# Twenty-four modulation products moved into the last attention pair, the mask made later, W_out staged under z's weights

## The chip, the core and the metric

The kernel runs on one core of a Trainium2 chip. The core has a matrix engine (TensorE, PE in the profile, with its weight loads as PEld), a vector engine (VectorE, DVE), a scalar engine (ScalarE, ACT), a general engine (GpSimd, POOL) and an engine that here only issues transfers (SyncE, SP). They share SBUF, the on-chip memory of 128 partitions; PE writes its results to a second memory, PSUM. Each engine takes its instructions in one fixed order and waits on semaphores where it needs another engine's result.

The metric is the time of one execution on the device, in microseconds. All arithmetic is in 32-bit floating point; a 32-bit matrix product is made here from three products of rounded parts (high times high, high times low, low times high).

## The reference

One layer of a hybrid encoder: 1024 tokens of width 1024. The parts that this case touches:

```python
mod = (c_act @ w_ada[l] + b_ada[l])[:, None, :]
sh_m, sc_m, g_m, sh_f, sc_f, g_f = jnp.split(mod, 6, axis=-1)      # six vectors of 1024
h = rmsnorm(x, norm_mix_w[l]) * (1 + sc_m) + sh_m
z, xbc, dt_raw, q, k, v = jnp.split(h @ w_in[l], IN_SPLITS, axis=-1)
y_ssd = ssd_mixer(z, xbc, dt_raw, ...)       # causal conv of width 4 and silu on xbc, scan in chunks, gate by silu(z), norm
y_att = chunk_attention(q, k, v, rel_bias[l])  # 8 heads of 64: own chunk of 64 tokens and the 8 before it
x = x + g_m * (jnp.concatenate([y_ssd, y_att], axis=-1) @ w_out[l])
h = rmsnorm(x, norm_ffn_w[l]) * (1 + sc_f) + sh_f
x = x + g_f * conv_ffn(h, w_up[l], ffn_conv_w[l], w_down[l])
...
return rmsnorm(x, final_norm_w)
```

The modulation `mod` is a product of a vector with a 1024 x 6144 matrix. The kernel makes it on VectorE, 128 columns at a time: 48 products in all, eight for each of the six vectors.

## The kernel before

The work runs in stages, and the code is written in that order, but the order on each engine is made by a scheduler: it lets work of a later stage slip in wherever buffers allow it by its own estimate of times. What the profile shows is that order.

1. The first 60 us load `x`, make the products for `SC_M` and `SH_M` and normalise. `hth` and `htl` are the rounded high part of h and the rest.
2. Attention runs over four pairs of heads. `qkp` is a pool of 12 tiles of 4 KB a partition; each pair takes six (`q`, `kh`, `kl` for two heads), so pairs 2 and 3 reuse those of 0 and 1. Inside a pair the loop over `u` takes two blocks of 128 queries at a time. `attn_scores` multiplies q with k into an `s` tile (there are two of these), adds the bias and finds the row's extreme on VectorE (L319), exponentiates on ScalarE (L322), takes the reciprocal of the row sum on VectorE (L324) and scales by it on GpSimd (L325). `attn_pv` transposes the result on PE, splits it into `pt` high and low (ScalarE and VectorE, L65 and L66) and multiplies with v; L367 and L368 add the halves up into `ya`.
3. The conv stage. `conv_silu` makes one of eight column tiles of `xbc`: `wu_pair` loads 512 KB of weights into one half of `raws` and splits them (ScalarE `wh`, GpSimd `wl`), `gemm_ft` does 48 products of 512 columns into an `s` tile, and VectorE runs three shifted multiply-adds from it (L415) and two halves of silu (L421). After each of the eight, three modulation products follow by `mods`: `mod_col` loads 512 KB of `w_ada` into one of three `mt` tiles, and VectorE multiplies with the row `rowa` and sums (L114). `tc.issue_after` keeps a product behind the conv's last VectorE instruction. They make `G_M`, `SC_F` and `SH_F`. The last four conv tiles are transposed into `xs` (L488).
4. The z stage: `wz_weights` loads and splits z's weights in two halves of four tiles, and `z_tile` makes 16 tiles of z. Eight more products by `mod_col` (`G_F`) stand ahead of it. Once `rowb` (the gate of the mixer, as a row in every partition) is made, `wout_weights` loads each of eight W_out tiles into `raws`, multiplies it by the gate (the fold, L511; `FOLD` says whether on GpSimd, 0, or VectorE, 1) and splits it into `wh`/`wl` or `woh`/`wol`.
5. The scan over eight chunks (`ssd_chunk`) together with the output product (`wout_tile`), then the feed-forward part from about 600 us to the end.

SP's transfers stand in one queue in program order; one that waits for a buffer holds up all behind it.

Of the kernel before, what the change touches and what calls it, by code (L numbers as in the profile page):

```python
# [10 lines left out]
F32 = mybir.dt.float32  # L11
# [15 lines left out]
PB = (2, 2, 1, 3)  # L27
FOLD = (0, 1, 0, 1)
PRST = 4
MTB = 3  # L30
GP, GPL = {0: (0,1), 2: (2,)}, ()
# [14 lines left out]
def tile_block(ctx: ExitStack, tc: tile.TileContext, x, crep, pk, w_ada, w_first, w_ft, w_z,  # L46
# [250 lines left out]
    def attn_scores(p, i, bt):  # L297
# [12 lines left out]
        for h in range(2):  # L310
            pt_ = p_tile()
            nm, rs = stat(), stat()
            if len(parts) == 1:
                src, bsl, dst = st[h][:, 0:n], bt[h][:, off:off + n], pt_[:, 0:n]
            else:
                src = st[h].rearrange("p (a b) -> p a b", a=2)[:, :, 0:320]
                bsl = bt[h].rearrange("p (a b) -> p a b", a=2)
                dst = pt_.rearrange("p (a b) -> p a b", a=2)
            V.tensor_tensor_reduce(out=dst, in0=src, in1=bsl, scale=-1.0, scalar=3e38,  # L319
                                   op0=ALU.add, op1=ALU.min, accum_out=nm)  # L320
            pv_ = pt_[:, 0:n]
            A.activation(pv_, pv_, AF.Exp, scale=-1.0, bias=nm, accum_out=rs)  # L322
            rr = stat()
            V.reciprocal(rr, rs)  # L324
            G.tensor_scalar(pv_, pv_, rr, None, op0=ALU.mult)  # L325
            res.append(pt_)
        return res

    def attn_pv(p, u, h, p0, p1):
# [12 lines left out]
        while done < nb:  # L342
# [16 lines left out]
            for bi, ((j, c0, n), o) in enumerate(bank):  # L359
# [10 lines left out]
                        tl.rearrange("p (a b) -> p a b", a=2), ALU.add)  # L370

    def attention(p, extra=()):
        extra = dict(extra)
# [7 lines left out]
        for u in range(4):  # L381
            pa = attn_scores(p, 2 * u, bt)
            pb = attn_scores(p, 2 * u + 1, bt)
            for fn in extra.get(u, ()):
                fn()
            for h in range(2):
                attn_pv(p, u, h, pa[h], pb[h])
# [20 lines left out]
    def conv_silu(ft, dst, th2):  # L408
        wh, wl = wu_pair(w_ft[ft], A, G)
        ps = s_tile()  # L410
# [15 lines left out]
    for p in (1, 2):  # L426
        attention(p, {u: [part(p + 1, w) for w in ws] for u, ws in GP.items()})
        for w in GPL:
            gemm_part(p + 1, w)
    attention(3)  # L430
    es_at.close()

# [24 lines left out]
    tle, ones = tle1[:, 0, :], tle1[:, 1, :]  # L457
    sgtr = bcp.tile([P, P], F32R, name="sgtr")
    sgt_ = th512()[:, 0:P]
    G.memset(ones, 1.0)  # L460
# [5 lines left out]
    sgt = f32(sgtr)  # L466
    na = bcp.tile([P, 16], F32, name="na")[:, 0:8]
    es_t = ExitStack()
    es_m = ExitStack()
    mtp = es_m.enter_context(tc.tile_pool(name="mtp", bufs=1, side="right", reuse_waits="tile"))  # L470

    def mt_tile():
        return mtp.tile([P, D], F32, tag="mt", bufs=MTB, name="mt")

    def mods(kt, at):
        for m in (G_M, SC_F, SH_F):
            mod_col(m + kt, mt_tile(), at)

    for g in range(2):
        mods(2 * g, conv_silu(4 + g, bt_[g], th512))  # L480
        mods(2 * g + 1, conv_silu(6 + g, ct_[g], th512))
    for ft in range(4):
        xt = bcp.tile([P, S], F32, tag="rm", bufs=2, name="xst")
        mods(4 + ft, conv_silu(ft, xt, th512))
        for hh in range(2):
            tps = tp_tile()
            for j in range(4):
# [3 lines left out]
                         tps.rearrange("p (a b) -> p a b", a=4), AF.Copy)  # L491
    mod_scale(affn, SC_F, NFFN, 0, KT)
    mod_shift(bffn, SH_F, 0, KT)
    wop_ = []
    halves = [slice(0, 512), slice(512, 1024)]
    order = [4, 5, 6, 7, 0, 1, 2, 3]

    def wout_weights(dh, js):
        ws = []
        for j in js:  # L500
# [14 lines left out]
        return ws  # L515

    es_m.close()

# [772 lines left out]
```

## Time and profile before

| | us |
|---|---|
| median of three runs (lowest, highest) | 1277.99 (1275.63, 1278.07) |
| the profiled execution | 1276.49 |
| its span, first to last instruction | 1274.8 |
| PE busy, share of the span | 1187.0, 93% |
| DVE busy | 960.0, 75% |
| ACT busy | 560.8, 44% |
| POOL busy | 199.0, 16% |
| mean granted PE clock | 0.975 |

The change touches the stretch from about 240 to 480 us: the last attention pair is in it from 244, the conv stage's products start at 274, z's at 395, the scan at 454. An engine that is mostly busy over the whole span can still stand idle in one stage, so the prediction reads this stretch in pieces. In the views of time the columns of each engine are its busy time in the piece and, in brackets, the number of instructions; "PEclk" is the granted clock of PE as a share of full speed.

### The profile page before, as it was taken

To read this page: it belongs to the slowest core of one execution; us is meant where nothing else is said; L and a number is where in the kernel's file an instruction comes from. 1 tells how busy PE (TensorE), PEld (TensorE's weight loads), DVE (VectorE), ACT (ScalarE), POOL (GpSimd) and SP (SyncE) were. 2 spreads that over 40 slices of the span, in tenths; PEclk is the share of its full clock that TensorE was granted. 3 is DMA by queue.
4 is the path that set the end of the run, shared out by engine and by line. 5 is a ranking of instruction groups with operands and counts; after the bars stand their busy time and mean duration, and the time that the engine had idled before them with its cause. 6 is when DMAs were issued, how large, how long until landed. Compare 5 with 4: busy or idle time off the path is not lost.

```text
span 1274.8 us, 15617 instructions
## 1 busy us (share of the span) xinstructions
PE 1187.0 (93%) x5786; PEld 992.2 (78%) x5786; DVE 960.0 (75%) x1448; ACT 560.8 (44%) x917; POOL 199.0 (16%) x178
## 2 busy tenths in 40 slices
PE   5898999999796979999889999999999999999995
PEld 3786888878686968888668888888888888888884
DVE  7927455554887786764989988888988879856976
ACT  4527455653322453423734445344445344433443
POOL 1305463661210242220000000000000000000002
PEclk9999999899897989999989999999999999999998
DMA  9702121100556222112113222333222195834433
GB/s 334 261 19 78 41 71 38 57 1 34 201 195 215 100 83 67 55 54 91 67 67 123 107 78 89 103 121 124 100 95 87 75 329 200 304 109 148 151 131 132
DMA packets 57835, 150.86 MB, mean 118 GB/s; under 512 B 5792, under 2 KB 5920, under 8 KB 56352
## 3 DMA queue, kind: packets, MB, share of 16 engines
q1 hardware_dynamic: 50704, 125.49, 29.2%
q10 hardware_dynamic: 7056, 24.38, 4.8%
q8 instruction: 45, 0.74, 0.2%
q14 instruction: 30, 0.25, 0.1%
HBM read 116.56 MB, written 29.10 MB: 114 GB/s over the span
## 4 chain that ended last, share of the span: by engine, by line
PE 79%; DVE 11%; ACT 4%; DMA 3%; issue 2%; POOL 1%; SPq 0%; DVEq 0%; POOLq 0%; ACTq 0%
PE dn L57 5%; PE dn L56 5%; PE dn L58 5%; PE uY L56 5%; PE uY L58 5%; PE uY L57 5%; PE uZ L56 3%; PE uZ L58 3%; PE uZ L57 3%; PE uX L56 3%; PE uX L57 3%; PE uX L58 3%; PE acc L56 3%; PE acc L57 3%; PE acc L58 3%; PE s L56 2%
## 5 line engine op out<-in xcount | busy, mean ns | idle before, releaser
L762 POOL TENSOR_TENSOR st<-st,mhalf 128x1 f32<-128x1 f32 x16 | 12.4, 777 | 681.6 <-DVE st L761 681.6
L56 PE MATMUL dn<-w 128*128 128x512 f32 x308 | 111.9, 389 | 0.0
L57 PE MATMUL dn<-w 128*128 128x512 f32 x308 | 111.9, 389 | 0.0
L58 PE MATMUL dn<-w 128*128 128x512 f32 x308 | 103.3, 389 | 0.0
L325 POOL TENSOR_SCALAR p<-p,st 128x640 f32<-128x640 f32 (+4 forms) x64 | 94.1, 1486 | 30.1 <-DVE st L324 26.3
L65 ACT ACTIVATE w<-ya 128x1024 fp32r<-128x1024 f32 (+1 forms) x44 | 41.8, 950 | 100.6 <-PE uY L58 93.2
L56 PEld LDWEIGHTS dn<-w 128*128 128x128 f32 x308 | 57.8, 188 | 12.1
L57 PEld LDWEIGHTS dn<-w 128*128 128x128 f32 x308 | 57.8, 188 | 12.1
L58 PEld LDWEIGHTS dn<-w 128*128 128x128 f32 x308 | 57.8, 188 | 11.9
L66 DVE TENSOR_TENSOR pt<-tp,pt 128x512 fp32r<-128x512 f32 (+2 forms) x72 | 41.9, 596 | 28.9 <-ACT pt L65 21.8
L65 ACT ACTIVATE w<-xs 128x1024 fp32r<-128x1024 f32 (+1 forms) x44 | 41.8, 951 | 41.1 <-PE uY L58 31.6
L319 DVE CUSTOM_DVE_ANT_0 p<-s,bias 128x640 f32<-128x640 f32 (+4 forms) x64 | 40.6, 651 | 24.7 <-PE tp L351 8.7
L56 PE MATMUL s<-hth,wh 128*128 128x512 f32 x128 | 51.3, 401 | 7.8 <-DVE ct L415 7.5
L65 ACT ACTIVATE pt<-tp 128x512 fp32r<-128x512 f32 (+2 forms) x72 | 36.4, 523 | 39.2 <-PE tp L351 19.8
L58 PE MATMUL s<-hth,wl 128*128 128x512 f32 x128 | 51.5, 402 | 0.0
L904 DVE SCALAR_TENSOR_TENSOR a<-cv,pkt,a 128x1023 f32<-128x1023 f32 (+1 forms) x40 | 51.1, 1276 | 0.1
L57 PE MATMUL s<-htl,wh 128*128 128x512 f32 x128 | 51.0, 399 | 0.0
L66 DVE TENSOR_TENSOR w<-ya,w 128x1024 fp32r<-128x1024 f32 (+1 forms) x44 | 47.7, 1084 | 4.4 <-ACT w L65 4.4
L322 ACT ACTIVATE p<-p,st 128x640 f32<-128x640 f32 (+4 forms) x64 | 44.1, 690 | 13.1 <-DVE st L319 12.9
L66 POOL TENSOR_TENSOR wl<-raws,wh 128x1024 fp32r<-128x1024 f32 x14 | 34.9, 2496 | 95.6 <-ACT wh L65 93.2
L904 DVE SCALAR_TENSOR_TENSOR a<-cg,pkt,a 128x1023 f32<-128x1023 f32 (+1 forms) x40 | 49.5, 1276 | 0.0
L66 DVE TENSOR_TENSOR w<-xs,w 128x1024 fp32r<-128x1024 f32 (+1 forms) x44 | 47.6, 1082 | 0.3 <-ACT w L65 0.3
(407 smaller groups left out, 3613.5 us busy)
## 6 DMA issues: line engine op xcount, KB each, us to landing
mt<-in_w_ada_dram SPq DMA_DIRECT2D x32, 512.0 KB, 4.5
gz<-a ACTq DMA_DIRECT2D x10, 1024.0 KB, 5.3
adat<-in_w_ada_dram SPq DMA_DIRECT2D x16, 512.0 KB, 5.8
ya<-in_w_up_dram SPq DMA_DIRECT2D x10, 768.0 KB, 4.0
xs<-in_w_up_dram SPq DMA_DIRECT2D x10, 768.0 KB, 4.0
raws<-in_w_ft_dram SPq DMA_DIRECT2D x14, 512.0 KB, 3.5
gy<-a ACTq DMA_DIRECT2D x10, 512.0 KB, 2.6
qk<-in_x_dram SPq DMA_DIRECT2D x8, 512.0 KB, 6.8
```

The lines of the kernel that those rows point to most:

```text
L56: T.matmul(ps, lh, rh, start=start, stop=False, skip_group_check=more)
L57: T.matmul(ps, lh, rl, start=False, stop=False, skip_group_check=more)
L58: T.matmul(ps, ll, rh, start=False, stop=stop, skip_group_check=more)
L65: i = A.activation(hi, src, AF.Copy) if ehi is A else ehi.tensor_copy(hi, src)
L66: return i, elo.tensor_tensor(lo, src, f32(hi), ALU.subtract)
L319: V.tensor_tensor_reduce(out=dst, in0=src, in1=bsl, scale=-1.0, scalar=3e38, op0=ALU.add, op1=ALU.min, accum_out=nm)
L322: A.activation(pv_, pv_, AF.Exp, scale=-1.0, bias=nm, accum_out=rs)
L325: G.tensor_scalar(pv_, pv_, rr, None, op0=ALU.mult)
L762: G.tensor_tensor(r, ms, mhalf[:, 0:1], ALU.pow)
L904: V.scalar_tensor_tensor(a[:, j:S], c[:, 0:S - j], w[2 - j], a[:, j:S], op0=ALU.mult, op1=ALU.add)
```

## The change

- The 24 products of `G_M`, `SC_F` and `SH_F` leave the conv stage. They are done inside `attention(3)`: after the scores of `u` = 1 four, of `u` = 2 four, of `u` = 3 sixteen (`MODS`), each behind the last reciprocal of those scores (`last_v`). Their `w_ada` tiles go into four of pair 2's six tiles in `qkp`, which are dead once pair 2's scores are done.
- The weights of the first two conv tiles are asked for inside that loop (`early`), ahead of the products in the code.
- `affn` and `bffn`, made from the products, move ahead of the last four conv tiles, and the mask (`tle`, `sgtr`) behind the first four.
- The eight products of `G_F` move from ahead of z into the last four conv tiles, two after each, on a new tile `wos` of 12 KB a partition; the pool of three `mt` tiles is gone.
- Three of the eight W_out tiles are then loaded into the three parts of `wos` and not into `raws`; all folds are on VectorE.

The first line numbers of the new file are three higher from `attention` on, and more after that.

```diff
-FOLD = (0, 1, 0, 1)
+FOLD = (1, 1, 1, 1)
+MODS = (0, 4, 4, 16)
-MTB = 3
...
-            V.reciprocal(rr, rs)
+            last_v[:] = [V.reciprocal(rr, rs).ins]
...
+    last_v, early = [], {}
+    mtq, todo = [], [(m + kt) for kt in range(KT) for m in (G_M, SC_F, SH_F)]
...
+            if p == 3:
+                if u < 2:
+                    early[4 + 2 * u] = wu_pair(w_ft[4 + 2 * u], A, G)
+                for _ in range(MODS[u]):
+                    mod_col(todo.pop(0), mtq[len(todo) % 4], last_v[0])
             for h in range(2):
                 attn_pv(p, u, h, pa[h], pb[h])
...
-        wh, wl = wu_pair(w_ft[ft], A, G)
+        wh, wl = early.pop(ft) if ft in early else wu_pair(w_ft[ft], A, G)
...
+    mtq += [qk_tile(F32) for _ in range(6)][2:]
     attention(3)
...
+    wos = bcp.tile([P, 3, D], F32, name="wos")
+    es_t = ExitStack()
+    for g in range(2):
+        conv_silu(4 + g, bt_[g], th512)
+        conv_silu(6 + g, ct_[g], th512)
+    mod_scale(affn, SC_F, NFFN, 0, KT)
+    mod_shift(bffn, SH_F, 0, KT)
...
-    for g in range(2):
-        mods(2 * g, conv_silu(4 + g, bt_[g], th512))
-        mods(2 * g + 1, conv_silu(6 + g, ct_[g], th512))
     for ft in range(4):
         xt = bcp.tile([P, S], F32, tag="rm", bufs=2, name="xst")
-        mods(4 + ft, conv_silu(ft, xt, th512))
+        at = conv_silu(ft, xt, th512)
+        for i in range(2):
+            mod_col(G_F + 2 * ft + i, wos[:, i, :], at)
...
-            t = raw_tile()
+            if (dh, j // 2) != (0, 0) and wosc[0] < 3:
+                t = wos[:, wosc[0], :]
+                wosc[0] += 1
+            else:
+                t = raw_tile()
...
-    for kt in range(KT):
-        mod_col(G_F + kt, bcp.tile([P, S], F32, tag="rm", bufs=2, name="mt"))
```

What the change does to the order is seen at three places. The first is VectorE in the last attention pair, from the scores of the fifth block of queries on (the 640-wide L319; `s`, `p`, `bias` and `st1` belong to the scores, `pt` and `ya` to the product with v). Before:

```order
L319 ISA p_2533,st1_72<-s_2519,bias_2372 128x640
L319 ISA st1_72 128x1
L324 RECIPROCAL st1_72<-st1_72 128x1
L368 TENSOR_TENSOR ya_828<-pv_2333,tl_2365 64x2x128
L319 ISA p_2548,st1_72<-s_2538,bias_2368 128x640
```

and now:

```order
L319 ISA p_2557,st1_72<-s_2543,bias_2378 128x640
L319 ISA st1_72 128x1
L324 RECIPROCAL st1_72<-st1_72 128x1
L114 ISA qk_2373,modc_71<-qk_2373,rows_67 128x1024
L114 ISA modc_71 128x1
L114 ISA qk_2372,modc_71<-qk_2372,rows_67 128x1024
L114 ISA modc_71 128x1
L114 ISA qk_2371,modc_71<-qk_2371,rows_67 128x1024
L114 ISA modc_71 128x1
L114 ISA qk_2370,modc_71<-qk_2370,rows_67 128x1024
L114 ISA modc_71 128x1
L368 TENSOR_TENSOR ya_828<-pv_2333,tl_2365 64x2x128
```

Four products stand in a row between the scores of the fifth and the sixth block; four more stand in the same way after the seventh block's first head, and sixteen behind the last reciprocal, between the pair's remaining `pt` splits.

The second place is VectorE in the conv stage, at the fifth conv tile (`xst` is the tile, L415 reads it out of PSUM, L421 ends it). Before:

```order
L415 SCALAR_TENSOR_TENSOR xst_3072<-s_3078,pkt_66,xst_3072 128x1023
L114 ISA mt_2996,modc_71<-mt_2996,rows_67 128x1024
L114 ISA modc_71 128x1
L421 SCALAR_TENSOR_TENSOR ct1_2753<-th_3057,ct1_2753 128x512
L421 SCALAR_TENSOR_TENSOR ct1_2753<-th_3060,ct1_2753 128x512
L114 ISA mt_3063,modc_71<-mt_3063,rows_67 128x1024
L114 ISA modc_71 128x1
L415 SCALAR_TENSOR_TENSOR xst_3072<-s_3078,pkt_66,xst_3072 128x1022
```

and now, where L423 and L429 are the same lines:

```order
L423 SCALAR_TENSOR_TENSOR xst_3091<-s_3097,pkt_66,xst_3091 128x1023
L423 SCALAR_TENSOR_TENSOR xst_3091<-s_3097,pkt_66,xst_3091 128x1022
L423 SCALAR_TENSOR_TENSOR xst_3091<-s_3097,pkt_66,xst_3091 128x1021
L63 SCALAR_TENSOR_TENSOR wzl_3419<-raws_68,wzh_3418 128x2x260
L429 SCALAR_TENSOR_TENSOR xst_3091<-th_3150,xst_3091 128x512
L429 SCALAR_TENSOR_TENSOR xst_3091<-th_3153,xst_3091 128x512
L114 ISA wos_2836,modc_71<-wos_2836,rows_67 128x1024
L114 ISA modc_71 128x1
```

The conv tile's own instructions now follow one another, z's first split (L63) comes already here, and two `G_F` products stand behind.

The third place is ScalarE where z ends and the output product begins (`woh` and `wol` are W_out's split tiles, `yh` the high part of `ya`). Before:

```order
L546 ACTIVATE zt<-s 128x260 x2
L65 ACTIVATE woh<-raws 128x1024 x2
L65 ACTIVATE yh<-ya 128x512
L696 ACTIVATE state_4056<-stp 128x512
L614 ACTIVATE th<-sg 128x512
```

and now:

```order
L551 ACTIVATE zt<-s 128x260
L65 ACTIVATE woh<-wos 128x1024 x3
L65 ACTIVATE woh<-raws 128x1024 x2
L65 ACTIVATE yh<-ya 128x512
L699 ACTIVATE state_4027<-stp 128x512
```

Five W_out splits, not two, stand ahead of the first `yh`.

More of the change, by code (lines that the diff above doesn't have):

```diff
@@ L458, in tile_block @@
     sgtr = bcp.tile([P, P], F32R, name="sgtr")
+    na = bcp.tile([P, 16], F32, name="na")[:, 0:8]
+    wos = bcp.tile([P, 3, D], F32, name="wos")
[5 more added lines that the diff above has]
+    mod_shift(bffn, SH_F, 0, KT)
     sgt_ = th512()[:, 0:P]
@@ L466, in tile_block @@
     sgt = f32(sgtr)
[L467 to L477, printed above, removed]
-    for g in range(2):
-        mods(2 * g, conv_silu(4 + g, bt_[g], th512))
-        mods(2 * g + 1, conv_silu(6 + g, ct_[g], th512))
     for ft in range(4):
         xt = bcp.tile([P, S], F32, tag="rm", bufs=2, name="xst")
-        mods(4 + ft, conv_silu(ft, xt, th512))
+        at = conv_silu(ft, xt, th512)
+        for i in range(2):
+            mod_col(G_F + 2 * ft + i, wos[:, i, :], at)
         for hh in range(2):
@@ L491, in tile_block @@
                          tps.rearrange("p (a b) -> p a b", a=4), AF.Copy)
-    mod_scale(affn, SC_F, NFFN, 0, KT)
-    mod_shift(bffn, SH_F, 0, KT)
     wop_ = []
+    wosc = [0]
     halves = [slice(0, 512), slice(512, 1024)]
@@ L515, in wout_weights @@
         return ws
-    es_m.close()
     def rm512():
```

## The prediction

> **What bounds the kernel now.** I read the page first, then the waits of PE in the stretch that the change touches, then that stretch in pieces, then the instructions around each wait. The page gives the whole:
>
> ```profile
> PE 1187.0 (93%) x5786; PEld 992.2 (78%) x5786; DVE 960.0 (75%) x1448; ACT 560.8 (44%) x917; POOL 199.0 (16%) x178
> ```
>
> PE is the bound over the span, so a change can win only what PE idles or does at a lower clock. The waits of PE between 328 and 412 us, the conv and early z stages, with total, times and longest:
>
> ```profile
> PE s L56 <- DVE ct L415: 7.5, 1, 7.5
> PE tp L488 <- DVE xst L421: 6.5, 1, 6.5
> PE zps L57 <- DVE wzl L63: 3.1, 1, 3.1
> PE zps L56 <- ACT wzh L62: 1.2, 1, 1.2
> ```
>
> Three of the four are for VectorE, the fourth for a split that had to wait for its place. Together PE stands 18.3 us. The pieces show the rest:
>
> ```profile
> 264.00:276.00 12.00, 10.83 (x69) 9.20 (x68) 11.09 (x35) 11.12 (x28) 10.79 (x7) 1.00 0.00 0
> 276.00:290.00 14.00, 14.00 (x76) 11.99 (x75) 3.01 (x6) 4.84 (x8) 8.22 (x5) 1.00 0.01 1
> 290.00:328.00 38.00, 38.00 (x208) 32.84 (x207) 17.99 (x22) 10.78 (x20) 6.97 (x6) 1.00 0.23 84
> 340.00:350.00 10.00, 2.54 (x8) 1.76 (x7) 10.00 (x12) 3.30 (x4) 2.34 (x1) 0.66 0.65 204
> 350.00:360.00 10.00, 10.00 (x39) 8.07 (x38) 9.24 (x15) 1.15 (x2) 0.00 (x0) 0.83 0.81 256
> 386.00:400.00 14.00, 3.31 (x13) 2.50 (x12) 12.91 (x22) 4.84 (x9) 0.00 (x0) 0.68 0.53 192
> 400.00:410.00 10.00, 9.91 (x66) 9.92 (x67) 6.05 (x12) 1.67 (x3) 0.00 (x0) 0.77 0.81 269
> 454.00:480.00 26.00, 19.03 (x86) 14.86 (x84) 23.75 (x24) 14.34 (x28) 14.16 (x9) 0.80 0.31 101
> ```
>
> The columns are PE, PEld, DVE, ACT and POOL busy, then the granted clock. From 340 to 350 and from 386 to 400 VectorE is full and PE nearly empty: here the 24 products sit. From 276 to 328 it is the other way round, PE full and VectorE at 21 of 52 us: room for 31 us of VectorE work. But in the twelve microseconds ahead of that, 264 to 276, the scores of the last attention pair, PE, VectorE, ScalarE and GpSimd are all at 90% or more. Two of the four places of the change lie in this tightest piece.
>
> **The gain in the conv stage.** After each long wait the clock is down, and PE works at the lower rate for a while: busy time by what the clock lacks is 2.54 x 0.34 + 10.00 x 0.17 + 3.31 x 0.32 + 9.91 x 0.23 = 5.9 us. With the 18.3 us of waits that is 24.2 us. I take all of it as gone: with 24 products out, a conv tile's own VectorE work is three L415 and two L421, and with two `G_F` products behind it
>
> ```profile
> 386.50 3.91 DVE L415 SCALAR_TENSOR_TENSOR xst<-s,pkt,xst 128x1023 f32<-128x1023 f32 x3 [2.38 <-ACT xst L413]
> 391.83 1.29 DVE L421 SCALAR_TENSOR_TENSOR xst<-th,xst 128x512 f32<-128x512 f32 x2
> 393.04 1.22 DVE L114 CUSTOM_DVE_ANT_0 mt<-mt,rows 128x1024 f32<-128x1024 f32 x1
> 394.18 1.22 DVE L114 CUSTOM_DVE_ANT_0 mt<-mt,rows 128x1024 f32<-128x1024 f32 x1
> ```
>
> 3.9 + 1.3 + 2 x 1.14 = 7.5 us (1.14 is the distance from one product to the next), against 48 products on PE, 10.9 us at the 0.227 us from one L57 to the next below. The transposes of each tile now stand some 45 matmuls behind its last, and z's splits come inside the conv stage. The bounds of this term are 18 (one wait stays in another form) and 25.
>
> **The cost in the attention pair.** What the score piece lets in is told by its end, the last reciprocal on VectorE and the first conv product on PE:
>
> ```profile
> 275.75 0.16 DVE L324 RECIPROCAL st<-st 128x1 f32<-128x1 f32 x1 [0.34 <-ACT p L322]
> 274.01 0.50 PE L56 MATMUL s<-hth,wh 128*128 128x512 f32 x1 [0.34 <-DVE st L319]
> 274.34 0.39 PE L57 MATMUL s<-htl,wh 128*128 128x512 f32 x1
> 274.57 0.40 PE L58 MATMUL s<-hth,wl 128*128 128x512 f32 x1
> 266.77 16.46 POOL L325 TENSOR_SCALAR p<-p,st 128x512 f32<-128x512 f32 x9 [0.71 <-DVE st L324]
> ```
>
> PE cannot start the conv stage earlier, since the conv tile takes an `s` tile that L319 has to free. So eight products ahead of the last L319 push PE's conv start out one for one: 8 x 1.14 = 9.1 us, if they run at their own speed. Behind them on VectorE stand L319 and the `pt` splits, and on these wait the next scores, the exponentials and the transposes; PE has nothing else in its order there. That is the lower bound of this term.
>
> They won't run at their own speed. GpSimd scales by L325 without a pause from 266.77 to 283.23, and the trace shows what VectorE does when GpSimd reads SBUF at the same time:
>
> ```profile
> 330.68 3.42 DVE L114 CUSTOM_DVE_ANT_0 mt<-mt,rows 128x1024 f32<-128x1024 f32 x1
> 330.62 2.40 POOL L66 TENSOR_TENSOR wl<-raws,wh 128x1024 fp32r<-128x1024 f32 x1 [2.65 <-ACT wh L65]
> 461.32 2.78 POOL L511 TENSOR_TENSOR raws<-raws,rows 128x1024 f32<-128x1024 f32 x1 [1.82 <-DVE xdt L591]
> 461.77 2.88 DVE L699 TENSOR_TENSOR yy<-yy,zs 128x512 f32<-128x512 f32 x1
> 464.06 1.49 POOL L592 TENSOR_TENSOR xdd<-xdt,ex 128x512 f32<-128x512 f32 x1
> 464.57 2.06 DVE L511 TENSOR_TENSOR raws<-raws,rows 128x1024 f32<-128x1024 f32 x1
> 465.56 1.17 POOL L96 TENSOR_SCALAR st<-st 128x1 f32<-128x1 f32 x1
> L96 POOL TENSOR_SCALAR st<-st 128x1 f32<-128x1 f32 x16 | 5.7, 356 | 76.2 <-ACT junk L210 41.6 <-ACT yt L701 34.6
> L325 POOL TENSOR_SCALAR p<-p,st 128x640 f32<-128x640 f32 x32 | 59.8, 1886 | 1.3 <-DVE st L324 1.0
> L319 DVE CUSTOM_DVE_ANT_0 p<-s,bias 128x640 f32<-128x640 f32 x8 | 6.5, 817 | 0.2 <-PE s L307 0.2
> ```
>
> A product that meets a GpSimd instruction takes 3.42 us and not 1.22, longer by nearly that instruction's 2.40. From 461 on the two take turns: L511 on GpSimd, then L699, then L592, then L511 on VectorE, then L96, which takes 1.17 us where its mean is 0.356. In the scores VectorE's inputs come from PSUM and SBUF, and L319 keeps its 0.82 us beside L325; the product reads both from SBUF. So I let a product wait for one L325 wherever one is due. The Trainium skill, page "SBUF — State Buffer", section "Who interferes with whom", has the rule: a VectorE instruction with two inputs in SBUF and a GpSimd instruction that reads SBUF shut each other out for their whole length. By that rule each of the eight that meets an L325 waits it out; by the page's other sentence, that one SBUF input does not contend, the scores are unharmed. The rows above agree, though for a scaling as long as L325 no run here shows it.
>
> The walk: the first four find one L325 due, of the fourth block's second head (its 512 wide: 16.46 - 8 x 1.886 = 1.4 us): 4 x 1.14 + 1.4 = 6.0. Then VectorE runs four L319 and the splits between, some 5 us, and releases four reciprocals; GpSimd gets through about one and a half of these scalings, so the second four meet the rest of one and two whole: 4 x 1.14 + 0.3 + 2 x 1.89 = 8.7. Together 14.7 us. The upper bound is a turn for each: 8 x (1.14 + 1.89) = 24.2. I take 14.7, since no more scalings are due. PE comes out of these waits at half clock, with the last scores, transposes and one v product (2 us at full clock) still ahead of the conv start: 1.7 us, bounds 0 to 4.
>
> Of the sixteen late products the first four, 4.6 us and two or three scalings, lie beside 37 conv matmuls, 8.4 us. The other twelve are paced by VectorE and their loads. A tile is free when its product is done, and the load takes
>
> ```profile
> mt<-in_w_ada_dram SPq DMA_DIRECT2D x32, 512.0 KB, 4.5
> ```
>
> 4.5 us, so four tiles give a product every (4.5 + 1.14) / 4 = 1.4 us, and twelve take 17 us. Between them stand the `pt` splits for which PE's v products wait. With 27, 21, 7 and 4 conv matmuls between these v products in PE's new order (59 x 0.227 = 13.4 us) and 3 us of v products and transposes, I find three waits of 1 to 1.5 us: 3.5 us, and 1.5 for the clock; bounds 0 and 9. By the time the third conv tile wants the first `s` tile back, the twelve are done.
>
> **The small parts.** The second bias tile of the pair is now issued behind three loads of 512 KB. At the 4.5 us of a load that is up to 4 us later, but VectorE has splits of the pair before to do meanwhile; 0.5 us, 0 to 3. The early weights stand where they stood on GpSimd and ScalarE: 0, the scheduler had them there. The mask is three instructions of 0.3 us, off the path: 0. The loads for the last conv weights are behind twenty product loads, done at about 320, and PE wants them at about 345: 0, covered by 25 us.
>
> At W_out's start PE waits today too:
>
> ```profile
> PE sg L612 <- ACT th L614: 2.9, 1, 2.9
> PE wops L56 <- ACT yh L65: 2.0, 1, 2.0
> PE wops L58 <- DVE yl L66: 1.6, 1, 1.6
> 454.69 1.99 ACT L65 ACTIVATE woh<-raws 128x1024 fp32r<-128x1024 f32 x2
> 456.58 0.62 ACT L65 ACTIVATE yh<-ya 128x512 fp32r<-128x512 f32 x1
> ```
>
> The folds leave GpSimd, and L699 no longer waits 2.2 us for one. Seven of eight are done in z, where VectorE has room. But five splits (5 x 1.0) now stand ahead of `yh` on ScalarE and five `wol` ahead of `yl` on VectorE: the first wait grows by 3 us, the later ones shrink by as much. I take 0, bounds -9 (all of these waits and their slow clock go: 6.5 + 19.03 x 0.2 = 10) and +3.
>
> **The sum**, on the profiled execution's 1276.49 us (its span is 1274.8): -24.2 + 14.7 + 1.7 + 5.0 + 0.5 + 0 = -2.3, so 1274.2. The median of the runs is 1.5 us above the profiled execution, so as a median 1275.7. What a measurement of this kernel can tell from no change is 0.2%, 2.6 us, so this stands at the edge. I forecast a small gain, most of it eaten in the attention pair.
>
> **The rivals.** (1) No turns: L325 and the product pass each other. For it: no row here shows an L325 that waits. Then the eight cost 9.1, half of the late waits go too (-2.5), and the time is 1275.7 - 8.1 = 1267.6. (2) Slower: GpSimd gets a turn between every two of the eight products, since the scalings of the fifth to seventh blocks pile up behind the first four. Place: the eight products; price 24.2 and not 14.7, so 1285. It decides from the point where the eight cost more than 14.7 + 2.3 + 2.6 = 19.6 us, five or more whole scalings between them; against it, only three to four are due by the walk. (3) W_out's waits go as the folds leave GpSimd: 1275.7 - 9 = 1267; against it, the five splits ahead of `yh`. (4) It doesn't do what it says: PE's waits at 340 and 386 come back, because an `s` tile or a transpose is late for another reason; 1275.7 + 18 = 1294. Against it, the order of VectorE in the conv stage.
>
> **How the numbers follow.** The walk as it stands: 0.57, alone 1269 to 1282; of this 0.26 faster, 0.17 same, 0.14 slower. Rival 1: 0.18, faster, with 0.01 of it same. Rival 2: 0.16, slower. Rival 3: 0.06, faster. Rival 4: 0.03, slower. So faster 0.49, same 0.18, slower 0.33. The range is 1264 to 1287: below it only rivals 1 and 3 together or the lower bounds at once, above it rival 4 and the worse half of rival 2.
>
> **What would show it.** In the profile after: PE's waits for L415, L421 and `wzl` are gone and the clock is 1.00 from about 328 to z's end; the two groups of four L114 are 6 and 9 us long, with products of about 3 us beside L325; the first conv product on PE comes at 289 to 292. If it comes at about 283, rival 1 holds; if later than 295, rival 2. The prediction is wrong if the products' loads come late, so that VectorE waits on DMA ahead of `pt` splits, or if z's stage shows a new wait of PE.

## The result, and the profile after

The changed kernel takes 1259.89 us (median of 4 runs, 1258.11 to 1260.77) against 1278.03 (4 runs, 1275.63 to 1279.03): a ratio of 0.9859, 95% interval 0.9842 to 0.9876. That is 18 us, or 1.4%, faster. 1275.7 was forecast, with a range of 1264 to 1287: the sign was right, the size far off. The profiled execution took 1259.93 us, its span is 1258.2.

The busy line of the page, then the pieces of the stretch that the prediction read, and PE's waits from 240 to 470 us (in total, times, longest; the last three stand at W_out's start, the rest of the list is below 1 us):

```profile
PE 1181.4 (94%) x5786; PEld 988.0 (79%) x5786; DVE 954.1 (76%) x1452; ACT 560.3 (45%) x917; POOL 196.6 (16%) x174
264.00:276.00 12.00, 7.44 (x43) 6.73 (x43) 11.94 (x29) 7.04 (x18) 8.44 (x5) 0.86 0.50 175
276.00:290.00 14.00, 10.15 (x47) 8.47 (x47) 13.10 (x30) 4.76 (x11) 14.00 (x5) 0.88 0.63 210
290.00:328.00 38.00, 35.74 (x184) 30.04 (x183) 33.09 (x53) 12.16 (x20) 8.84 (x4) 0.96 0.50 172
340.00:350.00 10.00, 10.00 (x46) 8.29 (x45) 4.10 (x4) 2.54 (x3) 2.40 (x1) 1.00 0.59 212
386.00:400.00 14.00, 14.00 (x109) 13.47 (x108) 9.48 (x17) 4.38 (x8) 0.00 (x0) 1.00 0.22 78
PE pv L362 <- DVE ya L368: 4.3, 1, 4.3
PE tp L351 <- DVE pt L66: 3.7, 1, 3.7
PE pv L363 <- DVE pt L66: 2.3, 2, 2.0
PE wops L56 <- ACT yh L65: 3.4, 2, 2.6
PE sg L615 <- ACT th L617: 2.1, 1, 2.1
PE wops L58 <- DVE yl L66: 1.0, 1, 1.0
```

The two holes of before, 340 to 350 and 386 to 400, are closed: PE is full there at clock 1.00. In their place there is a new, smaller hole from 264 to 290, where VectorE is full and PE waits once for each group of four products (4.3 and 3.7 us); behind the late ones it waits 2.0 us once. That is the exchange that was forecast. What was not forecast is its price. The groups themselves, on VectorE and beside them on GpSimd, and the first conv product on PE:

```profile
265.49 1.21 DVE L114 CUSTOM_DVE_ANT_0 qk<-qk,rows 128x1024 f32<-128x1024 f32 x1
266.62 1.22 DVE L114 CUSTOM_DVE_ANT_0 qk<-qk,rows 128x1024 f32<-128x1024 f32 x1
267.76 1.62 DVE L114 CUSTOM_DVE_ANT_0 qk<-qk,rows 128x1024 f32<-128x1024 f32 x1
269.32 1.21 DVE L114 CUSTOM_DVE_ANT_0 qk<-qk,rows 128x1024 f32<-128x1024 f32 x1
265.74 3.45 POOL L325 TENSOR_SCALAR p<-p,st 128x512 f32<-128x512 f32 x1 [0.66 <-DVE st L324]
272.09 21.97 POOL L325 TENSOR_SCALAR p<-p,st 128x640 f32<-128x640 f32 x8 [2.91 <-PE pv L363]
284.06 0.73 PE L56 MATMUL s<-hth,wh 128*128 128x512 f32 x1
```

The first four products take 5.0 us and not 6.0, the second four (274.91 to 279.47) 4.6 and not 8.7: but for one, which takes 1.62 us, they run at their own 1.14 us apart. It is the scaling that grew: L325 of 512 columns from 1.56 to 3.45 us, the eight of 640 from 8 x 1.886 = 15.1 to 22.0. PE begins the conv stage at 284.1, where 289 to 292 was forecast and 283 was the mark of the first rival.

To see where the whole difference lies I read when PE reaches five places, in each run's profiled execution: the first conv product, z's first and last, W_out's last, and the first product of the down part. Such marks come from one tile's instructions, first and last start:

```profile
L57 PE MATMUL zps<-wzl,hth x64: 278/282/586, 400.1 to 447.0; 128*128 128x260 f32 x64
L57 PE MATMUL zps<-wzl,hth x64: 279/282/286, 389.7 to 434.0; 128*128 128x260 f32 x64
```

The first row is before, the second after: z's last product stands at 447.0 and at 434.0. All marks in us:

| kernel | conv | z first | z last | W_out last | down first | span |
|---|---|---|---|---|---|---|
| before | 274.0 | 395.8 | 447.0 | 602.2 | 1051.1 | 1274.8 |
| after | 284.1 | 389.6 | 434.0 | 589.0 | 1034.5 | 1258.2 |
| before_no_products | 273.0 | 374.7 | 428.4 | 583.9 | 1031.0 | 1254.7 |
| after_no_products | 273.0 | 374.7 | 419.1 | 574.6 | 1020.1 | 1243.7 |
| none_in_scores | 274.6 | 396.6 | 441.0 | 596.5 | 1042.1 | 1265.8 |
| sixteen_in_scores | 283.9 | 386.7 | 431.1 | 586.1 | 1031.7 | 1255.3 |
| before_cg_first | 272.4 | 394.3 | 445.9 | 602.0 | 1048.3 | 1272.0 |
| before_folds_on_vector | 275.1 | 398.0 | 449.3 | 602.9 | 1050.0 | 1273.7 |
| after_folds_shared | 286.6 | 391.5 | 440.8 | 594.2 | 1039.9 | 1263.6 |
| after_without_wos | 285.7 | 391.0 | 437.2 | 589.1 | 1036.3 | 1259.9 |
| eight_to_conv | 274.1 | 387.0 | 431.4 | 586.5 | 1032.0 | 1255.7 |
| twelve_to_conv | 275.7 | (353.5) | 424.5 | 580.3 | 1027.5 | 1251.2 |

(In the last kernel a few z products slip in early, hence the brackets.) A single mark carries some scatter: the first score product of PE, which no edit here touches, comes between 101.0 and 105.1 us, and the conv start of the eight kernels with no product between the scores lies between 272.4 and 275.7. The same eight products between the scores give a conv start of 284.1 in the change, 285.7 in after_without_wos and 286.6 in after_folds_shared. Differences of one stage's length are steadier than the marks. From before to after, stage by stage: +10.1 to the conv start, -16.3 in the conv stage, -6.8 in z, -0.2 in the scan and W_out, -3.4 in the feed-forward part up to the down products, 0 behind: -16.6.

### The profile page after: what moved, and what is told of

Same layout as the page of the kernel before. It is cut to its first block, busy times and chain, and to the rows that moved or that the text cites. A ratio compares the mean times of both kernels' runs of the same rounds, so it can differ in the third digit from the quotient of the medians.

```text
span 1258.2 us, 15608 instructions
## 1 busy us (share of the span) xinstructions
PE 1181.4 (94%) x5786; PEld 988.0 (79%) x5786; DVE 954.1 (76%) x1452; ACT 560.3 (45%) x917; POOL 196.6 (16%) x174
## 4 chain that ended last, share of the span: by engine, by line
PE 80%; DVE 11%; ACT 3%; issue 2%; DMA 2%; POOL 0%; SPq 0%; DVEq 0%; POOLq 0%; ACTq 0%
PE dn L57 6%; PE dn L56 6%; PE dn L58 5%; PE uY L56 5%; PE uY L58 5%; PE uY L57 5%; PE uZ L58 3%; PE uZ L57 3%; PE uZ L56 3%; PE uX L58 3%; PE uX L57 3%; PE uX L56 3%; PE acc L56 3%; PE acc L57 3%; PE acc L58 3%; PE wops L56 2%
## 5 line engine op out<-in xcount | busy, mean ns | idle before, releaser
L325 POOL TENSOR_SCALAR p<-p,st 128x640 f32<-128x640 f32 (+4 forms) x64 | 103.0, 1623 | 31.5 <-DVE st L324 26.2
L319 DVE CUSTOM_DVE_ANT_0 p<-s,bias 128x640 f32<-128x640 f32 (+4 forms) x64 | 40.6, 650 | 23.5 <-PE tp L351 8.7
L66 DVE TENSOR_TENSOR pt<-tp,pt 128x512 fp32r<-128x512 f32 (+2 forms) x72 | 41.9, 596 | 20.4 <-ACT pt L65 13.3
L66 DVE TENSOR_TENSOR w<-ya,w 128x1024 fp32r<-128x1024 f32 (+1 forms) x44 | 47.8, 1087 | 5.1 <-ACT w L65 5.1
L66 POOL TENSOR_TENSOR wl<-raws,wh 128x1024 fp32r<-128x1024 f32 x14 | 33.9, 2422 | 89.0 <-ACT wh L65 89.0
L66 DVE TENSOR_TENSOR w<-xs,w 128x1024 fp32r<-128x1024 f32 (+1 forms) x44 | 47.7, 1085 | 0.0
```

The costliest lines, as they stand in the source:

```text
L66: return i, elo.tensor_tensor(lo, src, f32(hi), ALU.subtract)
```

## The experiments

Ratios are to the kernel before, with the 95% interval; the changed kernel's own is 0.9859. On the scale of its 1278.0 us for before, 0.001 is 1.3 us.

### turns_alone: what a product and a GpSimd instruction cost each other

A kernel with nothing of the layer in it, only the two engines beside each other:

```
both(prod, 8, no, 0)        # products alone
both(no, 0, scal, 8)        # scalings 128x640 alone
both(prod, 24, scal, 8)
both(no, 0, sub, 6)         # subtractions 128x1024, two SBUF inputs
both(prod, 24, sub, 6)
both(score, 24, scal, 8)    # scores: PSUM and SBUF
...
both(mul, 32, scal, 8)
```

> This kernel does nothing of the layer; it only sets VectorE and GpSimd beside one another in six stretches, each behind a fence: 8 modulation products alone; 8 scalings (128x640, one input in SBUF) alone; 24 products beside 8 scalings, both queues full; 6 GpSimd subtractions (128x1024, two inputs in SBUF) alone, and beside 24 products; 24 score instructions (PSUM and SBUF) beside 8 scalings; products with a pause behind each beside scalings; 32 products of 128x512 of two SBUF tiles beside 8 scalings. Theory A (VectorE goes ahead: a product that follows a product directly leaves GpSimd no turn): the 24 products keep 1.14 to 1.3 us each, 27 to 31 us in all, and the 8 scalings, 15 us alone, stretch by about as much as the products that run beside them. Theory B (turns, the prediction's): 24 products beside 8 scalings take 27 + 15 = 42 us, each of the first eight 3 us. Theory C (no exclusion between the two): 27 us and 15 us side by side. The change's profile, with a median of 1.21 us a product and 2.76 us a scaling, speaks for A; a product of 1.6 us among them speaks against a clean A.

The timeline of both engines; L74 is the product, L88 the scaling, L91 the subtraction:

```profile
34.49 14.92 POOL L88 TENSOR_SCALAR p<-p,one 128x640 f32<-128x640 f32 x8 [31.04 <-ACT row L69]
52.07 31.62 POOL L88 TENSOR_SCALAR p<-p,one 128x640 f32<-128x640 f32 x8 [2.66 <-ACT row L69]
52.03 1.23 DVE L74 CUSTOM_DVE_ANT_0 mt<-mt,row 128x1024 f32<-128x1024 f32 x1 [20.13 <-ACT row L69]
53.18 1.22 DVE L74 CUSTOM_DVE_ANT_0 mt<-mt,row 128x1024 f32<-128x1024 f32 x1
54.33 1.73 DVE L74 CUSTOM_DVE_ANT_0 mt<-mt,row 128x1024 f32<-128x1024 f32 x1
86.45 13.83 POOL L91 TENSOR_TENSOR wl<-raw,wh 128x1024 f32<-128x1024 f32 x6 [2.76 <-ACT bia L69]
102.73 18.73 POOL L91 TENSOR_TENSOR wl<-raw,wh 128x1024 f32<-128x1024 f32 x6 [2.45 <-ACT bia L69]
102.90 3.25 DVE L74 CUSTOM_DVE_ANT_0 mt<-mt,row 128x1024 f32<-128x1024 f32 x1 [19.22 <-ACT row L69]
106.08 3.35 DVE L74 CUSTOM_DVE_ANT_0 mt<-mt,row 128x1024 f32<-128x1024 f32 x1
145.77 14.92 POOL L88 TENSOR_SCALAR p<-p,one 128x640 f32<-128x640 f32 x8 [24.31 <-ACT row L69]
```

Beside scalings, two products run at 1.14 us, the third takes 1.73, and so on, every third, to the end: 24 products in 31.6 us, 0.51 us lost for each of eight scalings. The scaling pays: 3.95 us each and not 1.87. Beside subtractions it is the other way round: each of the first six products takes 3.35 us, a loss of 2.13, while a subtraction goes from 2.31 to 3.12. Scores beside scalings cost neither anything (14.92 us for eight, as alone). Two further stretches are not in these rows: products with a pause of some 1 us behind them lost nothing (1.21 us each), while the scalings took 3.20 us; the 32 multiplications of 128x512 took 0.73 us each and the scalings 2.93, but these multiplications were not run alone. So none of the three theories holds as it stood. A is nearest for scalings, though a scaling costs every third product 0.5 us; B, the prediction's, is near for the subtraction and fails for the scaling. The two GpSimd instructions differ in how many inputs they read from SBUF (two and one), and also in operation and size; which of these sets the price was not tried.

### before_no_products and after_no_products: the gain and the cost, each alone

In both the 24 products and their loads are left out (the three vectors are zero).

```diff
 # before
     def mods(kt, at):
-        for m in (G_M, SC_F, SH_F):
-            mod_col(m + kt, mt_tile(), at)
+        pass
 # after
-                    mod_col(todo.pop(0), mtq[len(todo) % 4], last_v[0])
+                    pass
```

> The kernel before without the 24 products of G_M, SC_F and SH_F and without their loads (those three vectors are left at zero); all else stands as it was. It measures the gain term by itself, the whole of what the products cost in the conv stage. By the prediction's term, 18.3 us of waits and 5.9 us of lower clock: 1278.0 - 24.2 = 1253.8. The order of VectorE at the feed-forward part's start is here that of the changed kernel (cg ahead of the weight split), which by the change's profile gives 3.3 us more: 1250.5. If the conv stage's gain is smaller since other work is late there, 1258 to 1262.

> The changed kernel without the 24 products of G_M, SC_F and SH_F and without their loads (the three vectors are left at zero); early weights, wos, folds and G_F products stay. The difference to the changed kernel (1259.9) is what the products cost in their new place. By the stage account of the change's profile (conv start 10.0 us later, with some 1 us of work done earlier, and 3.5 to 4 us lost behind it) this is 12.5 to 14: 1246 to 1247.5 us. Rival, from before_no_products at 1255.9 (then the products cost only 4 us in their new place and the rest of the gain was never to be had): 1254 to 1257. Whatever comes, its difference to before_no_products (1255.9) is the worth of the other parts: G_F products, wos, folds, mask.

Measured: 1255.87 us, 0.9837 (0.9823 to 0.9852), and 1245.21 us, 0.9754 (0.9739 to 0.9768). Without the products the conv stage takes 101.7 us in both (273.0 to 374.7), against 121.8 before: the products cost 20.1 us there in their old place. But z gets 2.5 us longer without them (53.7 against 51.2), and the feed-forward part is 1.8 us shorter and not 3.3: before_no_products is 20.8 us faster than the kernel before by the ratio, where its expectation had 27.5 (24.2 and 3.3), so that expectation missed. In the new place they cost 0.9859 - 0.9754 = 0.0105 of the time, 13.4 us; by the marks the conv start comes 11.1 us later and the conv and z stages together take 149.9 us and not 146.1, 3.8 us more. The expectation of 12.5 to 14 held, that of the rival (4 us) did not. The two kernels differ by 0.0083, 10.6 us, with none of the 24 products in either: that is the worth of the other edits. Most of it lies in z, 53.7 us in the one and 44.4 in the other. In before_no_products the eight `G_F` products still stand in z, one with VectorE idle 1.98 us ahead of it for its load, and from 399 to 402 us PE waits for a z tile behind it:

```profile
PE s L56 <- DVE zs L550: 3.4, 1, 3.4
```

Then it is busy 4.0 us at a granted clock of 0.60, so this place costs some 5.0 of the 9.3 us; after_no_products has no wait in z.

### none_in_scores and sixteen_in_scores: how many products between the scores

```diff
-MODS = (0, 4, 4, 16)
+MODS = (0, 0, 0, 24)     # none_in_scores
+MODS = (0, 8, 8, 8)      # sixteen_in_scores
```

> The changed kernel with all 24 products behind the pair's last reciprocal, none between the scores. Theory A (each product between scores pushes the conv start out by its own 1.14 us): the first conv product comes at 274 to 275 us and not 284.1. What is then lost later: sixteen late products took 26.6 us (284.6 to 311.2), so 24 take 40 us, to 315, and the first s tile is free at about 319; PE has two conv tiles (22 us) and 10 us of v work till then, so it waits 10 to 13 us and comes out at half clock: about 1262 us, no better than the change (1259.9). Rival (the late products are hidden whatever their number): 1250. Rival of the prediction (eight products cost 15 to 17 us in the scores and the rest lies elsewhere): 1245 to 1250.

> The changed kernel with sixteen products between the scores of the last pair and eight behind them. Theory A: the first conv product at 284.1 + 8 x 1.14 = 293 us, one for one, and 2 to 3 us saved behind it since only eight products are late: 1266 to 1267 us. Theory B (turns, with GpSimd's backlog growing as more products come): the second eight cost 2 to 3 us each, conv start at 300 to 308, 1275 to 1280 us.

None: 1265.98 us, 0.9913 (0.9897 to 0.993), 7 us slower than the change. The conv start is at 274.6, as expected. Then PE waits, from 270 to 330 us:

```profile
PE s L56 <- DVE bt L423: 7.4, 1, 7.4
PE pv L363 <- DVE pt L66: 5.3, 2, 4.9
```

The 12.7 us agree with the 10 to 13 expected, but the clock was undersized: from 300 to 328 us PE is busy 14.5 us at a granted clock of 0.68, which is 4.6 us more. Against after_no_products the conv and z stages lose 20.3 us here. Sixteen late products cost 3.8 us, twenty-four 20.3.

Sixteen: 1260.12 us, 0.9867 (0.9852 to 0.9883), the same as the change, where 1266 was expected. The conv start is at 283.9 and not 293. VectorE's last two scores of the pair are

```profile
283.06 0.82 DVE L319 CUSTOM_DVE_ANT_0 p<-s,bias 128x640 f32<-128x640 f32 x1
285.02 0.82 DVE L319 CUSTOM_DVE_ANT_0 p<-s,bias 128x640 f32<-128x640 f32 x1
```

and the conv start lies between them: behind a first four the scheduler put the products singly and in pairs between the scores, and only eleven of the sixteen stand ahead of it. Eleven cost 9.9 us here and eight 10.1 in the change, 0.9 and 1.3 us each; with the scatter of the marks that agrees with a product's own 1.14 us, and it settles the price no closer. "One for one with the number asked for" was wrong; one for one with those that truly stand ahead is not contradicted.

### before_cg_first: the order at the feed-forward part's start

The changed kernel is 3.4 us faster in a part that the change does not touch. PE's wait there is 3.1 us before and 1.6 after, for `cg`; VectorE's rows ahead of it before (first four) and after (last three):

```profile
648.57 1.21 DVE L66 TENSOR_TENSOR t4l<-a,t4h 128x1024 fp32r<-128x1024 f32 x1
649.71 1.21 DVE L66 TENSOR_TENSOR w<-xs,w 128x1024 fp32r<-128x1024 f32 x1
650.84 0.68 DVE L856 TENSOR_TENSOR ya<-ya 128x512 f32<-128x512 f32 x1
651.44 1.27 DVE L882 TENSOR_TENSOR cg<-cv,uY 128x512 f32<-128x512 f32 x2
635.35 1.23 DVE L66 TENSOR_TENSOR t4l<-a,t4h 128x1024 fp32r<-128x1024 f32 x1
636.48 0.69 DVE L885 TENSOR_TENSOR cg<-cv,uY 128x512 f32<-128x512 f32 x1
637.08 1.23 DVE L66 TENSOR_TENSOR w<-xs,w 128x1024 fp32r<-128x1024 f32 x1
```

The scheduler has put `cg` ahead of a split and a sum. To test that this order is the cause, the kernel before got the split (and it alone) behind the first `cg` (`cgi[0]`):

```diff
                 if p not in u.w and p != "P3":
-                    u.prep(p, order[n + 1])
+                    with tc.issue_after(cgi[0]) if q == 0 and p == "Q7" and u is units[1] else ExitStack():
+                        u.prep(p, order[n + 1])
```

> The kernel before with one change of order at the feed-forward part's start: the 1024-wide split of xs for the Q7 and Q4 products waits its turn behind the first cg (L882), as the scheduler orders it in the changed kernel; all else as before. Theory (order at that place is worth the 3.3 us by which the changed kernel is faster there): PE's wait of 3.08 us for cg becomes 3.08 - 1.14 = 1.9 us, too short for the clock to fall, which saves 1.5 us more: 1277.3 - 2.6 = 1274.7. Rival (the split is late instead, or the 3.3 us come from the scan's end and not from the order): 1277 to 1278.

1272.72 us, 0.9975 (0.996 to 0.9991), 3.2 us faster. From W_out's last product to the first of the down part it takes 446.3 us, 2.6 less than before's 448.9, as expected; the change takes 445.5. PE begins again twice here, after a wait for a split (`w`) and after the one for `cg`:

```profile
640.01 0.76 PE L58 MATMUL uZ<-t1h,w 128*128 128x512 f32 x1 [3.08 <-DVE w L66]
652.26 0.47 PE L56 MATMUL uY<-t3h,w 128*128 128x512 f32 x1 [3.08 <-DVE cg L882]
626.80 0.79 PE L58 MATMUL uZ<-t1h,w 128*128 128x512 f32 x1 [3.07 <-DVE w L66]
637.32 0.47 PE L56 MATMUL uY<-t3h,w 128*128 128x512 f32 x1 [1.60 <-DVE cg L885]
```

From the one to the other it is 12.25 us before (first two rows) and 10.52 after (last two); in before_cg_first it is 11.12. So the order gives the change 1.7 us directly, and the rest because the shorter wait for `cg` (1.60 us) brings no slow clock behind it: before, eight products from 653.7 to 657.1 us come 0.43 us apart and not 0.23, which is 1.6 us. It is a side effect: `cg` stands ahead of the split in all of the other kernels here too, whatever was changed in them.

### before_folds_on_vector, after_folds_shared: the folds

```diff
-FOLD = (0, 1, 0, 1)
+FOLD = (1, 1, 1, 1)      # before_folds_on_vector; after_folds_shared is the reverse, in the changed kernel
```

> The kernel before with all eight folds on VectorE (FOLD), nothing else of the change. Its order at the feed-forward part's start is the changed kernel's, worth 2.6 to 3.3 us. The prediction's term for W_out's start was 0: then 1277.3 - 3 = 1274.3. Its third rival (W_out's waits go as the folds leave GpSimd) gives 1277.3 - 3 - 9 = 1265; folds that make VectorE late in z, where the 24 and 8 products already are: 1278 to 1282.

> The changed kernel with the folds shared between GpSimd and VectorE as before (FOLD 0, 1, 0, 1). From z's end to W_out's last product the change's profile takes 155.1 us and that of before 155.2, and with only the folds changed (before_folds_on_vector) 153.6. Theory (folds on VectorE are worth 0 to 2 us, since ScalarE's five splits ahead of yh hold PE back, not the folds): 1260 to 1262 us, no difference that can be told. Rival (a GpSimd fold with two SBUF inputs takes full turns with VectorE, 3.3 us for each, at the time when yl is due): 1264 to 1268.

In the kernel before: 1272.47 us, 0.9967 (0.9953 to 0.9982): by the marks 1.8 us of it in the feed-forward part, 1.6 in the scan and W_out, z unchanged. The 4.2 us are near the 3 expected, and the 12 of the third rival are excluded. In the changed kernel, folds shared again: 1264.3 us, 0.9905 (0.989 to 0.9919), 5.9 us slower by the medians' ratio. The theory of 0 to 2 us fell; the rival's time is right, but not its place: z takes 49.3 us and not 44.4, the scan and W_out 153.4 and not 155.0, so the two together lose 3.3 us. (In the profiled execution the conv start is another 2.5 us later, before any fold runs.) Of the 4.9 us in z, 2.5 are waits of PE and the other 2.5 mostly work of the scan that PE does there already (it is busy 46.9 us and not 44.4). In z, GpSimd's folds and what VectorE does beside them:

```profile
417.17 4.73 POOL L518 TENSOR_TENSOR wos<-wos,rows 128x1024 f32<-128x1024 f32 x2 [46.52 <-ACT rows L125]
417.30 2.36 DVE L561 SCALAR_TENSOR_TENSOR sm_p<-zs 128x64 f32<-128x64 f32 x1
419.58 2.87 DVE L121 TENSOR_TENSOR gt<-ident,gcol 128x512 f32<-128x512 f32 x1
PE rowps L124 <- DVE gt L121: 1.2, 1, 1.2
PE zps L56 <- DVE zs L552: 1.0, 1, 1.0
```

An instruction of 128x64 takes 2.36 us (0.22 in the kernel before) and one of 0.69 us (the L121 just ahead of them) 2.87, each beside one fold; PE then waits for `gt` and for a z tile's evacuation. That is what the subtraction did to products in turns_alone. It is the price of folds on GpSimd in the changed kernel; in the kernel before, moving them to VectorE left z as long as it was (51.3 and 51.2 us).

### after_without_wos: the staging

```diff
-            if (dh, j // 2) != (0, 0) and wosc[0] < 3:
+            if (dh, j // 2) != (0, 0) and wosc[0] < 0:
```

> The changed kernel with all W_out tiles through raws, none staged in wos (G_F's products still use it). The loads of three more tiles then wait for the two halves of raws, so fewer splits are done by the time PE asks for W_out. Theory (the splits, not the loads, are what W_out's start waits for, and fewer of them stand ahead of the first yh): -2 to +2 us, 1258 to 1262. Rival (without the staging the woh and wol tiles are late and PE waits for them): 1264 to 1270.

1262.75 us, 0.99 (0.9869 to 0.9931), four runs from 1258.76 to 1267.17: against the change that is 1 to 9 us, and the change's own interval overlaps it, so this is not decided. In the profiled execution z is 1.8 us longer, the scan and W_out 3.1 shorter, the feed-forward part 1.7 longer (a slow clock behind `cg`, in the same order). Nothing in it shows a large worth of the staging.

### eight_to_conv and twelve_to_conv: a better place

The runs say that products between the scores cost their own time, that sixteen late ones cost little and twenty-four much; and after 328 us the change's VectorE has room. So none between the scores, fewer late, the rest behind the first four conv tiles, in the parts of `wos`:

```diff
-MODS = (0, 4, 4, 16)
+MODS = (0, 0, 0, 16)     # eight_to_conv, with n = 2; twelve_to_conv: (0, 0, 0, 12), n = 3
...
-        conv_silu(4 + g, bt_[g], th512)
-        conv_silu(6 + g, ct_[g], th512)
+        for ft, dst in ((4 + g, bt_[g]), (6 + g, ct_[g])):
+            at = conv_silu(ft, dst, th512)
+            for _ in range(n):
+                mod_col(todo.pop(0), wos[:, len(todo) % 3, :], at)
```

> A version made from the readings: no product between scores, sixteen behind the pair's last reciprocal, and eight behind the first four conv tiles, two each, in the three parts of wos. From 328 to 386 us the changed kernel's VectorE is busy 36 of 58 us, so eight products (9 us) fit there. Conv start at 274.6 as in none_in_scores; the third conv tile's s tile is free eight products (12 us) earlier than there, so its waits of 7.4 and 5.5 us go down to 2 to 4: 1266.0 - 10 - 2 = 1252 to 1255 us, 5 to 8 us below the changed kernel. Rival (the room on VectorE is not at the right place, or wos's space comes free only with the last scores' tiles at 345, so that the eight are late and push z): 1258 to 1264.

> As eight_to_conv, with twelve products behind the pair's last reciprocal and twelve behind the first four conv tiles, three each. In eight_to_conv PE waits 5.6 us at 305 to 311 for a pt split that stands behind the last two late products (one of them 2.8 us beside a GpSimd subtraction) and three L423, and 1.2 us before it. With four fewer there these waits go (6.8 us and 3 us of lower clock), if VectorE's 60 of 86 us between 300 and 386 can take four more products (4.6 us): 0.976 to 0.978 of the kernel before, 1247 to 1250 us on the scale where the change has 1259.9. Rival (three products per conv tile delay L423 or L429 as they did in the kernel before): 1255 to 1262.

Eight: 1255.46 us, 0.9833 (0.9808 to 0.9858), 3.3 us below the change by the ratios, where 5 to 8 were expected; the two intervals overlap, so this is not decided. Conv start 274.1, but against after_no_products 11.2 us are lost behind it, and PE waits 6.8 us where 2 to 4 were expected. The first two rows are PE's wait and its place in eight_to_conv, the last is the longest wait of PE in twelve_to_conv from 255 us to the scan:

```profile
PE pv L363 <- DVE pt L66: 6.8, 2, 5.6
310.73 0.48 PE L363 MATMUL pv<-pt,v 128*128 128x128 f32 x1 [5.60 <-DVE pt L66]
PE s L56 <- DVE xst L423: 1.0, 1, 1.0
```

Twelve: 1247.72 us, 0.9785 (0.9761 to 0.9809), clear of the change's interval: 9.5 us faster than it; 0.976 to 0.978 was expected. The long waits are gone, conv and z take 148.8 us, 2.7 more than with no products at all, and the rival (conv instructions late again with three products a tile, as in the kernel before) shows as one wait of 1.0 us. This kernel is faster than the one before and the change.

## Why the prediction was wrong, step by step

The exchange was read rightly: two waits of PE in the conv stage for two in the scores, the clock at 1.00 from 328 to z's end, conv start set by the products ahead of the last L319, no second wait in z. Its terms were not. (The line "here the 24 products sit" is loose: they run from 329 to 395 us, and only some six start in the two pieces that it names. No term rests on it.)

- **"So I let a product wait for one L325 wherever one is due."** This is the step that failed. The rows it rested on were GpSimd instructions with two SBUF inputs (L66, L511, L592) and a scaling one column wide; L325 reads one wide input. turns_alone gives 0.51 us for a scaling, where 1.89 went into the sum. The eight products took 9.6 us of VectorE, not 14.7, so only some 0.5 us of the 5.6 for scalings came. With clock and bias tile the conv start moved 10.1 us (11.1 against after_no_products; up to 12.6 in the other two kernels with these eight), where the sum had 14.7 + 1.7 + 0.5 = 16.9. Rival 1 had the right mark (283) by half the right reason: nothing is free, but GpSimd pays, with 6.9 us on the eight long scalings, and none of PE's long waits names it. The Trainium skill, page "SBUF — State Buffer", which the prediction weighed, says in section "SBUF: two separate sides" that whichever of the two starts first has the shared pair of ports for its whole instruction and the other is blocked, and in section "Who interferes with whom" that the order of issue decides. The measured 0.51 us and 2.09 us for one pair, at full queues on both sides, differ from that, and the measurement decides; for the product and the subtraction (2.13 and 0.82) the first part is near.
- **"Bounds 0 and 9", 5.0 us late.** Measured 3.8: the size was right. The form was one wait of 2.0 us and slower work behind it, not three waits of 1 to 1.5.
- **The gain of 24.2.** By the marks, 18.3 of it lay ahead of z's first product (waits of 7.5, 6.5 and 1.2, clock 3.1) and 5.9 behind. With no products the whole change takes 146.1 us for conv and z, where the kernel before takes 173.0: 26.9, above the upper bound of 25. In the conv stage that is 20.1, of which 15.2 are the waits; PE is busy 106.7 us there before and 101.7 in after_no_products, by the slow clock and by the last eight transposes, which come behind z's first product in after_no_products. z gave 6.8, in after_no_products as in the change (51.2 to 44.4): the wait of 3.1, and 3.7 of busy time. Taking the products out was not enough for it: before_no_products gains only 17.6 in conv and z, since `G_F`'s products in z hold PE up as told above.
- **W_out's start: 0.** By the marks -0.2, and PE's waits there add up to 6.5 us as before. But the folds' term was looked for in the wrong stage: in the changed kernel, folds on GpSimd would cost z 2.5 us of waits, by after_folds_shared.
- **No term for the feed-forward part.** The sum stopped at W_out. The order there was changed too, and the order of the two programs, which could be had before any run, shows it; I had read it only at the places that the diff names. 3.4 us.
- **The sum.** Forecast -2.3 on the profiled execution, measured -16.6: 6.8 from the scores, 3.0 from the conv stage (-18.3 + 5.0 forecast, -16.3 measured), 0.9 from z, 0.2 from W_out, 3.4 from the feed-forward part, 14.3 in all. So the failed step is nearly half of the miss. Below 1264 the prediction saw only rivals 1 and 3 together or all lower bounds at once; rival 3 did not come. The range left no room for a gain outside the stretch.

What stays open: why the scheduler turned the order at the feed-forward part's start was not tried; what the staging alone is worth is not decided; and how VectorE and GpSimd come to the shares that turns_alone shows is not known.

## What to carry to other kernels

A price of contention belongs to the two instructions on which it was measured; take it from a row with the same two forms, or measure that pair by itself before it decides a sum. Where a scheduler makes the order, compare the orders over the whole program: a change may move a wait hundreds of microseconds behind its last line. And look for VectorE's room in the stage where PE is full: by their place, the same 24 products put z's last product off by 18.6 us (the kernel before), 14.9 (the change) or 5.4 (twelve_to_conv), each against its kernel without them.

## What the runs showed of the hardware

At full queues on both sides, a GpSimd scaling of 128x640 (one SBUF tensor in) lost 2.09 us to products and cost them 0.51; a GpSimd subtraction of 128x1024 (two in) lost 0.82 us and cost each product beside it 2.13. A short VectorE instruction pays as well: one of 128x64 took 2.36 us beside a fold, where it took 0.22 in the kernel before.

The clock behind a wait of one length is not always the same. before_folds_on_vector has the changed kernel's order, and waits of 3.07 and 2.96 us at the two places shown above:

```profile
640.70 0.50 PE L58 MATMUL uZ<-t1h,w 128*128 128x512 f32 x1 [3.07 <-DVE w L66]
641.03 0.39 PE L56 MATMUL uZ<-t1h,w 128*128 128x512 f32 x1
651.21 0.47 PE L56 MATMUL uY<-t3h,w 128*128 128x512 f32 x1 [2.96 <-DVE cg L882]
652.67 0.63 PE L56 MATMUL uY<-t3h,w 128*128 128x512 f32 x1
656.07 0.39 PE L58 MATMUL uY<-t3h,w 128*128 128x512 f32 x1
```

Behind the first it works on at the full rate (0.39 us a product), where before and the change had a slow start (0.76 and 0.79) behind the same wait; behind the second the slow rate (0.63) comes 1.5 us after the work has begun again, and lasts 3.4 us. So a wait near 3 us may cost some 1.6 us more or not, and a kernel's time moves by that from edit to edit. The Trainium skill, page "TensorE: Matmul & The Clock Gate", Part 1, tells of a window of about 3.4 us that runs freely and judges whether PE was idle in it; the slow stretch of 3.4 us and its start at no fixed time behind the wait agree with such a window. The page lets the clock fall after a whole idle window; the waits here, 2.96 to 3.08 us, are shorter than that and the clock fell all the same, so there the measurement decides.
